# A sigmoid-gate projection computed as four more groups of a seven-product matmul loop, with the residual strips built one stage later

## The chip, the cores and the metric

The kernel runs on one core of a Trainium2 chip. The metric is the device time of one execution in microseconds. A core has a matmul engine (TensorE, PE in the profile; its weight loads are listed as PEld), three engines for element work (VectorE or DVE, ScalarE or ACT, GpSimd or POOL), and SyncE (SP), which here only issues DMAs. Each engine runs its own instructions in order; they wait for one another through semaphores. SBUF is the on-chip memory with 128 partitions, PSUM is the memory that PE writes to, and DRAM lies outside the core.

## What is computed

One step of a one-layer decoder, for a prompt of 512 tokens and 8 single-token samples with the same weights: 520 token columns in all. The input projection, the mLSTM, the window attention and the first LayerNorm end in a vector `x` of 1024 features for each token. What follows is what the change touches:

```python
g, u = jnp.split(x @ w_gate_up, 2, axis=-1)          # 1024 -> 2 x 2816
ffn = (jax.nn.silu(g) * u) @ w_down                  # 2816 -> 1024
ple = jax.nn.sigmoid(x @ w_ple_gate) * (p @ w_ple)   # 1024 -> 1024, the "gate"
x = layer_norm(ALPHA * x + ffn + ple, ln2_g, ln2_b)
```

All data are float32.

## The kernel before

**Layout.** Activations lie with features on the partitions: a matrix of 1024 features is 8 strips of 128 x 520. [...] Each float32 operand is split into a high part (rounded to fp32r by an ACT copy) and a low part (the rest, a DVE subtraction; both in `split`, L216 and L217). A product is three matmuls: high x high, high x low, low x high. The normalised input of this stage is `x1hi`, `x1lo`, in the slabs T0 and T1.

**Weights.** `load_next` (L163) brings weight blocks of up to 1 MB into the ring `raw` of two buffers, from SP's queue; a block's load waits until the buffer's last reader is done. A block of 256 columns is two pieces of 128. `get(k)` returns piece k split, and has pieces k+1 and k+2 split ahead of time into the rings `whi` and `wlo` (3 buffers each).

**The stages at the end, in order.**

1. `w_gate_up`. The first `BSW` = 2 of its 11 column blocks of 256 are done classically (`mm3ab`, L243). The other nine, gate and up part alternating, are the 18 entries of the list `sw`, the groups of the *seven-product loop* (L1703). It treats a group of 256 output rows, 1024 inputs and 520 columns as 2 x 2 blocks, and forms the four output blocks from seven block products instead of eight (`ORDER`: a11, s4, s1, s2, a22, a12, s3). A product is 4 k-blocks x 3 = 12 matmuls of 260 columns (L1600); one step of the loop is one product. Weight blocks come as four loads of 256 KB a group (`st_load`, L176). `w_sum` forms the sums of weight blocks on DVE, `w_hi` and `w_lo` split them (L1579, L1584), `harvest` combines results: ACT seeds a PSUM bank from another, DVE adds two terms (L1689, L1694), and `put_g` or `put_h` takes the finished block. `put_g` applies Silu on ACT (L1618) and keeps the result in the ring `gt` (5 buffers); `put_h` multiplies it with the up part on DVE (L1629) and splits the product into `hhi`, `hlo`, the input of the down projection. Strips 16 to 21 of it can't be split yet: their place is taken by sums of activations that the loop reads (`tf`). They stay unsplit in `h6`, in slab T2.
2. The *gate stage* (L1731), eight row blocks of 128 done classically, 48 matmuls each. For each, ACT takes tanh(z/2) from PSUM (`sig_gate`, L1168), and DVE builds the residual strip `base[f]` in three operations for each half (L1740 to L1742): (tanh + 1) times half of `p @ w_ple`, plus ALPHA x1hi, plus ALPHA x1lo. Half of `p @ w_ple` was written to the DRAM tile `plesc` at the start of the kernel and is brought back by SP (L1729). The six strips of `h6` are split here as well.
3. The *down projection* (L1783). For three blocks b of two output rows each, the 22 input strips are taken in three parts g of 8, 8 and 6 (`KG`), two pieces a each: 18 pieces, then 3 pieces for row 6, then row 7, whose second half is interleaved with the output stage. After a row's last piece `ev_d` adds the strip to PSUM on DVE (L1762), PE transposes the sum (L1771), ACT copies it to `R2` (L1772), and DVE takes statistics (L1780).
4. The output stage: the second LayerNorm over tokens and the stores.

**What sets the order.** Inside `tc.manual_schedule` (the loop, the output stage) the order of PE, DVE, ACT and POOL is that of the program text. Elsewhere, and for SP's queue everywhere, a planner orders each engine's instructions with its own model of time; on the chip every queue then runs strictly in that order. A tile of a ring or slab can be taken when all readers of its predecessor are done.

Of the kernel before, what the change touches and what calls it, by code (L numbers as in the profile page):

```python
# [9 lines left out]
F32 = mybir.dt.float32  # L10
# [7 lines left out]
P = 128  # L18
# [32 lines left out]
def tile_hybrid_step(  # L51
# [25 lines left out]
    def psm():  # L77
        return pm.tile([P, 512], F32, tag="m", name=nm("psm"))
# [7 lines left out]
    def ring(tag, n, bufs, p=P):  # L86
        return wp.tile([p, n], F32, tag=tag, name=nm(tag), bufs=bufs)
# [3 lines left out]
    def slab(i):  # L91
        return up.tile([P, U], F32, tag=f"T{i}", name=nm(f"T{i}_"))
# [4 lines left out]
    def v3(t):  # L97
        t3 = t[:, : KD * NT].rearrange("p (j c) -> p j c", j=KD)
        return [t3[:, j, :] for j in range(KD)]
# [38 lines left out]
    def add_block(src, kc, ncol, pcol=P):  # L138
        bi_ = len(blocks)
        blocks.append((src, kc, ncol))  # L140
        first = len(pieces)
        for a in range(0, ncol, pcol):
            pieces.append((bi_, a, kc, pcol, a + pcol >= ncol))
        return first
# [66 lines left out]
    def get(k, ahead=2):  # L211
        prep_to(k + ahead)
        return ready.pop(k)

    def split(hi, lo, src, le=None):
        S.activation(rr(hi), src, AF.Copy)  # L216
        (le or V).tensor_tensor(rr(lo), src, hi, ALU.subtract)  # L217
# [18 lines left out]
    def mm3ab(pss2, parts, total=None, begin=0):  # L236
        tot = total if total is not None else sum(3 * p[3] for p in parts)
        i = begin
        for hi, lo, wc, kc, ah, al, k0 in parts:
            for k in range(kc):  # L240
                for w, a in ((hi, ah), (hi, al), (lo, ah)):
                    for ps, (c0, n) in zip(pss2, HALVES):
                        T.matmul(  # L243
                            ps[:, :n],
                            rr(w[:, k, wc : wc + P]),
                            rr(a[k0 + k][:, c0 : c0 + n]),
                            start=(i == 0),
                            stop=(i == tot - 1),
                        )
                    i += 1  # L250
        return i
# [41 lines left out]
    for b in range(11):  # L293
        for c0 in (0, DFF):
            src = w_gu2[:, c0 + 256 * b : c0 + 256 * (b + 1)]
            if b < BSW:
                add_block(src, KD, 256)
            else:
                sw.append((src, b, c0 > 0))
    k_sw = len(blocks)  # L300
    blocks.extend([None, None])
    k_pg = len(pieces)
    for b in range(4):
        add_block(w_pg[0][:, 256 * b : 256 * (b + 1)], KD, 256)
    k_dn = len(pieces)
    KG = ((0, 8), (8, 8), (16, 6))
    for b in range(3):
# [85 lines left out]

    pT = [[strip(2 + 2 * i + k) for k in range(2)] for i in range(2)]
    plesc = dp.tile([P, KD, NT], F32, tag="plesc", name="plesc")

    def ple_p():
        for hf, (c0, n) in enumerate(HALVES):
# [767 lines left out]
    def sig_gate(psx, n):  # L1166
        th = ring("th", 264, 3)
        S.activation(th[:, :n], psx[:, :n], AF.Tanh, scale=0.5)  # L1168
        return th
# [244 lines left out]
    def part(w):  # L1414
        return [(w[0], w[1], 0, KD, x1hi, x1lo, 0)]
# [194 lines left out]
    def later(s, kind, f):  # L1610
        todo.setdefault((s, kind), []).append(f)
# [10 lines left out]
    def put_h(s, b, r, hf, src, sc=1.0, own=None):  # L1622
# [7 lines left out]
        if f < 16:  # L1630
            hi, lo = (x[f // 8][f % 8][:, c0 : c0 + TH] for x in (hhi, hlo))
            later(s + 1, "act", lambda: S.activation(rr(hi), h, AF.Copy))
            later(s + 2, "dve", lambda: V.tensor_tensor(rr(lo), h, hi, ALU.subtract))

    pz = {}

    def product(s):
# [17 lines left out]

    def harvest(s):
        g, form = steps[s - 1]
        _, b, up = sw[g]
        put = put_h if up else put_g

        def seed(f):
            later(s, "seed", f)

        if form == "a11":
            pb, pa = pss(), pz[g, "a"]
            pz[g, "b"] = pb
            if g < 2:
                prime(pb)
            seed(lambda: S.activation(pb[:, :TH], pa[:, :TH], AF.Copy))
        elif form == "s1":  # L1670
            p5, pc = ring("th", 264, 3), pz[g, "c"]
            pz[g, "p5"] = p5
            seed(lambda: S.activation(p5[:, :TH], pc[:, :TH], AF.Copy))
        elif form == "s2":
            pb, pd, u1 = pz.pop((g, "b")), psm(), ring("th", 264, 3)
            pz[g, "d"], pz[g, "u1"] = pd, u1
            if g < 2:
                prime(pd)
            seed(lambda: S.activation(pd[:, :TH], pb[:, :TH], AF.Copy))
            seed(lambda: S.activation(u1[:, :TH], pb[:, :TH], AF.Copy))  # L1680
        elif form == "a12":
            put(s, b, 0, 0, pz.pop((g, "a"))[:, :TH])
        elif form == "a22":
            put(s, b, 1, 0, pz.pop((g, "d"))[:, :TH], -1.0)
        else:
            x = ring("tmp", 264, 4) if up else ring("gt", 264, 5)
            xs = x[:, :TH]
            if form == "s3":
                V.scalar_tensor_tensor(  # L1689
                    xs, pz[g, "d"][:, :TH], -1.0, pz.pop((g, "p5"))[:, :TH], ALU.mult, ALU.subtract  # L1690
                )
                put(s, b, 1, 1, xs, own=x)
            else:
                V.tensor_tensor(xs, pz.pop((g, "c"))[:, :TH], pz.pop((g, "u1"))[:, :TH], ALU.add)  # L1694
                put(s, b, 0, 1, xs, own=x)
# [23 lines left out]
            if 0 <= s < ns:  # L1719
                product(s)  # L1720

    base = v3(h5)[6:]
    for k, hx in ((2, hlo), (3, hhi)):
        ta, tb = slab2(k, "h5")
        hx.append([ta[:, i * NT : (i + 1) * NT] for i in range(KF - 16)])
        base += [tb[:, i * NT : (i + 1) * NT] for i in range(2)]
    base += [ring("stg", NT, 2) for _ in range(2)]
    for f in range(KD):
        nc.sync.dma_start(base[f], plesc[:, f, :])  # L1729

    for f in range(KD):  # L1731
        w = get(k_pg + f)
        p2 = (psm(), psm())
        mm3ab(p2, part(w))
        if 1 <= f < 7:
            split(hhi[2][f - 1], hlo[2][f - 1], h6[f - 1])
        for psx, (c0, n) in zip(p2, HALVES):
            th = sig_gate(psx, n)
            bs = base[f][:, c0 : c0 + n]
            V.scalar_tensor_tensor(bs, th[:, :n], 1.0, bs, ALU.add, ALU.mult)  # L1740
            V.scalar_tensor_tensor(bs, x1hi[f][:, c0 : c0 + n], ALPHA, bs, ALU.mult, ALU.add)
            V.scalar_tensor_tensor(bs, x1lo[f][:, c0 : c0 + n], ALPHA, bs, ALU.mult, ALU.add)  # L1742

    R2 = slab(0)[:, : NCH * D].rearrange("p (c d) -> p c d", c=NCH)
    t1n = slab(1)
    ysm = t1n[:NS, :D]
    l2g = t1n[:, D : 2 * D]
    l2b = t1n[:, 2 * D : 3 * D]
    st2 = t1n[:, 3 * D : 3 * D + 192].rearrange("p (c f s) -> p c f s", c=NCH, f=KD)
    RS = t1n[:, 3 * D + 192 : 3 * D + 256].rearrange("p (f b) -> p f b", f=KD)  # L1750
    RQ = t1n[:, 3 * D + 256 : 3 * D + 320].rearrange("p (f b) -> p f b", f=KD)
    rss = t1n[:, 3 * D + 320 : 3 * D + 336].rearrange("p (a b) -> p a b", a=2)
    nc.scalar.dma_start(l2g, ln2_g[0].partition_broadcast(P))
    nc.scalar.dma_start(l2b, ln2_b[0].partition_broadcast(P))

    def dpart(g, w):
        return [(w[0], w[1], 0, KG[g][1], hhi[g], hlo[g], 0)]

    def ev_d(f, hf, psx):
        c0, n = HALVES[hf]  # L1760
        r2 = ring("tmp", 264, 4)
        V.tensor_tensor(r2[:, :n], psx[:, :n], base[f][:, c0 : c0 + n], ALU.add)  # L1762
        if hf == 0:
            G.tensor_copy(RS[:, f, :], r2[:, :NS])  # L1764
        return r2

    def ev_dt(f, hf, r2):
        ps = pss()
        o = NS if hf == 0 else 0
        for i in range(2):  # L1770
            T.transpose(ps[:, i * P : (i + 1) * P], r2[:, o + i * P : o + (i + 1) * P], ident)  # L1771
        S.activation(  # L1772
            R2[:, 2 * hf : 2 * hf + 2, f * P : (f + 1) * P],
            ps[:, : 2 * P].rearrange("p (c d) -> p c d", c=2), AF.Copy,
        )
        return ps
# [6 lines left out]
    for b in range(3):  # L1783
        pps = [(psm(), psm()) for _ in range(2)]
        cnt = [0, 0]
        for g in range(3):
            for a in range(2):
                w = get(kp)
                kp += 1
                cnt[a] = mm3ab(pps[a], dpart(g, w), total=3 * KF, begin=cnt[a])  # L1790
                if g == 2:
                    for hf in range(2):
                        f = 2 * b + a
                        ev_ds(f, hf, ev_dt(f, hf, ev_d(f, hf, pps[a][hf])))
# [11 lines left out]
    for g in range(3):  # L1806
        ws.append(get(kp, 1))
        kp += 1
        cnt = mm3(pa, HALVES[0], dpart(g, ws[g]), total=3 * KF, begin=cnt)

    h0, h1, q3 = slice(0, 512), slice(512, D), slice(768, D)

    def mmb(k0, k1):
# [156 lines left out]
```

## Time and profile before

| | us |
|---|---|
| three timed runs | 897.55, 898.10, 898.61 |
| median | 898.1 |
| the profiled execution | 900.21 |
| its span, first to last instruction | 898.2 |
| mean granted PE clock | 0.99 |

| stage, in the span | from | to |
|---|---|---|
| seven-product loop, on PE | 525 | 709 |
| gate stage, on PE | 705 | 753 |
| down projection | 753 | 875 |
| output stage | 875 | 898 |

(The loop's last product and the gate stage's first matmuls are interleaved on PE.) In the profile, L12 is line 12 of the kernel. A row of instructions gives line, engine, operation, output and input by their names, shape and count, then busy time and mean length; in brackets stands how long the engine was idle before and who ended that. A row of stretches gives for each engine the busy time and in brackets the number of instructions. A list of waits gives total, number and longest.

### The profile page before, as it was taken

The page shows a single profiled execution, that of the slowest core. Times are in us where ns is not written, and L with a number is a line of the kernel's source. Part 1 is how long each engine was busy: PE and PEld are TensorE (multiplying, and loading weights), DVE is VectorE, ACT ScalarE, POOL GpSimd, SP SyncE. Part 2 cuts the span into 40 slices and gives each one's busy share as a digit, 9 for nine tenths or more (in the row PEclk, how much of TensorE's full clock was granted, in tenths as well). Part 3 has the DMA queues.
Part 4 walks back from the last instruction along what each step waited for, and adds up shares of the span by engine and source line. Part 5 has one row for each costly group of instructions (what it writes and reads, how often), then busy time and mean ns, then how long its engine had stood idle before and what let it go on. Part 6 is the DMA issues. An engine that isn't in the chain of part 4 may idle for free.

```text
span 898.2 us, 18486 instructions
## 1 busy us (share of the span) xinstructions
PE 873.0 (97%) x7130; PEld 860.3 (96%) x7130; DVE 637.4 (71%) x1547; ACT 466.6 (52%) x1102; POOL 159.2 (18%) x320
## 2 busy tenths in 40 slices
PE   8999899999999999999999999999999999999994
PEld 7999899999999899999999999999999999999993
DVE  7788555688888777778877978999988654223327
ACT  6545254657777655557326656666665522212212
POOL 5441321115464411311014100000000000000004
PEclk9999999999999999999999999999999999999997
DMA  7642631336465441121710333333332723322212
GB/s 240 212 151 71 188 102 54 55 112 148 144 174 169 142 141 49 53 90 48 235 48 1 90 100 100 101 114 107 99 106 73 229 87 123 103 94 71 66 41 96
DMA packets 118039, 99.42 MB, mean 111 GB/s; under 512 B 6410, under 2 KB 112610, under 8 KB 117928
## 3 DMA queue, kind: packets, MB, share of 16 engines
q1 hardware_dynamic: 117520, 96.94, 36.0%
q8 instruction: 56, 0.92, 0.4%
q10 hardware_dynamic: 432, 1.31, 0.4%
q14 instruction: 31, 0.25, 0.1%
HBM read 89.01 MB, written 10.34 MB: 111 GB/s over the span
## 4 chain that ended last, share of the span: by engine, by line
PE 85%; DVE 6%; DMA 3%; ACT 3%; issue 1%; POOL 1%; SPq 0%; DVEq 0%; ACTq 0%; POOLq 0%
PE psm L243 46%; PE psm L1600 12%; PE pss L1600 9%; PE psm L226 6%; PE pss L683 2%; DMA big<-vsd 1%; PE psm L467 1%; PE pss L736 1%; PE pss L720 1%; PE psm L1428 1%; PE pss L1069 1%; PE pss L1073 1%; ACT T L1371 1%; DMA out_dram<-stg 1%; DMA T<-in_w_ple_dram 1%
## 5 line engine op out<-in xcount | busy, mean ns | idle before, releaser
L243 PE MATMUL psm<-T,whi 128*128 128x264 f32 x2000 | 346.5, 286 | 0.6 <-DVE Qbd L670 0.4
L243 PEld LDWEIGHTS psm<-T,whi 128*128 128x128 f32 x2000 | 284.7, 189 | 2.6 <-PE pss L1147 0.6
L243 PE MATMUL psm<-T,wlo 128*128 128x264 f32 (+1 forms) x1056 | 230.0, 288 | 1.5 <-DVE wlo L217 1.5
L217 DVE TENSOR_TENSOR wlo<-raw,whi 128x1024 fp32r<-128x1024 f32 (+1 forms) x86 | 104.8, 1218 | 107.2 <-ACT whi L216 106.8
L243 PEld LDWEIGHTS psm<-T,wlo 128*128 128x128 f32 x1056 | 168.1, 189 | 2.4 <-DVE wlo L217 1.7
L216 ACT ACTIVATE whi<-raw 128x1024 fp32r<-128x1024 f32 (+1 forms) x86 | 89.1, 1038 | 154.5 <-PE psm L243 139.6
L1764 POOL COPY T<-tmp 128x8 f32<-128x8 f32 x8 | 1.5, 190 | 376.4 <-DVE tmp L1762 376.4
L708 POOL TENSOR_SCALAR g<-g,sm 128x256 f32<-128x256 f32 (+1 forms) x64 | 36.2, 578 | 80.3 <-DVE sm L706 24.2
L243 PE MATMUL psm<-L,whi 128*128 128x264 f32 x224 | 45.0, 282 | 0.0
L701 ACT ACTIVATE g<-g,sm 128x256 f32<-128x256 f32 (+1 forms) x64 | 30.2, 474 | 19.3 <-DVE sm L697 18.2
L217 POOL TENSOR_TENSOR gt<-big,gt 128x256 fp32r<-128x256 f32 x32 | 27.5, 868 | 55.2 <-ACT gt L216 36.1
L1584 DVE TENSOR_TENSOR whi<-raw,whi 128x512 fp32r<-128x512 f32 x45 | 30.9, 687 | 8.5 <-ACT whi L1579 7.6
L1579 ACT ACTIVATE whi<-raw 128x512 fp32r<-128x512 f32 x45 | 28.3, 628 | 15.9 <-PE psm L1600 12.8
L1579 ACT ACTIVATE wlo<-raw 128x512 fp32r<-128x512 f32 x45 | 28.3, 630 | 13.6 <-ACT gt L1618 8.8
L243 PEld LDWEIGHTS psm<-L,whi 128*128 128x128 f32 x224 | 34.3, 188 | 0.0
L1584 DVE TENSOR_TENSOR wlo<-raw,wlo 128x512 fp32r<-128x512 f32 x45 | 30.9, 686 | 3.7 <-ACT wlo L1579 3.3
L1600 PE MATMUL psm<-tf,whi 128*128 128x260 f32 x228 | 30.3, 282 | 0.0
L692 DVE CUSTOM_DVE_ANT_0 g<-pss,amaskA,sink 128x256 f32<-128x256 f32 (+1 forms) x64 | 26.1, 444 | 4.0 <-PE pss L683 2.5
L1600 PE MATMUL psm<-T,wlo 128*128 128x260 f32 x216 | 28.9, 283 | 0.0
L1600 PE MATMUL pss<-tf,whi 128*128 128x260 f32 x216 | 28.9, 283 | 0.0
L1600 PE MATMUL pss<-tf,wlo 128*128 128x260 f32 x216 | 28.9, 283 | 0.0
L1600 PE MATMUL psm<-T,whi 128*128 128x260 f32 x216 | 28.9, 283 | 0.0
(446 smaller groups left out, 2007.8 us busy)
## 6 DMA issues: line engine op xcount, KB each, us to landing
raw<-in_w_in_dram SPq DMA_DIRECT2D x24, 1024.0 KB
raw<-in_w_gate_up_dram SPq DMA_DIRECT2D x72, 256.0 KB
raw<-in_w_down_dram SPq DMA_DIRECT2D x6, 1024.0 KB
big<-in_state_mlstm_C_dram SPq DMA_DIRECT2D x8, 512.0 KB
big<-vsd SPq DMA_DIRECT2D x8, 512.0 KB
out_dram<-big SPq DMA_DIRECT2D x8, 512.0 KB
raw<-in_w_out_dram SPq DMA_DIRECT2D x4, 1024.0 KB
raw<-in_w_gate_up_dram SPq DMA_DIRECT2D x4, 1024.0 KB
```

Of the source, the lines that this page charges most:

```text
L216: S.activation(rr(hi), src, AF.Copy)
L217: (le or V).tensor_tensor(rr(lo), src, hi, ALU.subtract)
L226: T.matmul(ps[:, :n], rr(w[:, k, wc : wc + P]), rr(a[k0 + k][:, c0 : c0 + n]), start=(i == 0), stop=(i == tot - 1),)
L243: T.matmul(ps[:, :n], rr(w[:, k, wc : wc + P]), rr(a[k0 + k][:, c0 : c0 + n]), start=(i == 0), stop=(i == tot - 1),)
L467: T.matmul(t01[t][hf][:, :n], rr(w[:, k, :]), rr(x[k][:, c0 : c0 + n]), start=(k == 0 and i == 0), stop=(k == KD - 1 and i == 2),)
L683: T.matmul(sc[:, a, :w], rr(q[:, a, n * P : (n + 1) * P]), rr(KS[:, kv, hl, (n - 1 + k0) * P : (n + 1) * P]), start=(hl == 0), stop=(hl == 1),
L692: V.tensor_tensor_reduce(out=pr[:, a, :w], in0=sc[:, a, :w], in1=amaskA[:, k0 * P :], scale=1.0, scalar=sink8[:, 2 * j + a : 2 * j + a + 1 ...
L701: S.activation(pr[:, a, :w], pr[:, a, :w], AF.Exp, bias=sm[:, 2 + a : 3 + a], scale=ASC, accum_out=sm[:, 8 + a : 9 + a],)
L708: G.tensor_scalar(pr[:, a, :w], pr[:, a, :w], sm[:, 12 + a : 13 + a], 0.5, ALU.mult, ALU.mult)
L1579: S.activation(rr(t[:, 0]), wsrcs[i], AF.Copy)
L1584: V.tensor_tensor(rr(lo), wsrcs.pop(i), hi, ALU.subtract)
L1600: T.matmul(ps[:, :TH], rr(w[:, j, :]), rr(x[j]), start=(start and j == 0 and i == 0), stop=(j == 3 and i == 2), skip_group_check=not start,)
```

## The change

The four column blocks of `w_ple_gate` are no longer pieces of a classical stage. They are groups 18 to 21 of the seven-product loop, with a third way of taking a finished block, `put_p`: tanh on ACT into a buffer of the ring `gt`, then a DMA from SP into a new DRAM tile `thsc`. The gate stage is gone. The strips are built in the down projection by `mkbase`, ahead of the matmuls of a piece that the table `bases` names (i counts pieces 0 to 17): tanh and `plesc` are loaded for each half, then the same three DVE operations follow. The splits of `h6` come ahead of pieces 0 to 2. Since `x1hi` and `x1lo` are read longer, `R2` moves from slab T0 to T2, the rows of the second LayerNorm are loaded to T1 at piece 12 by SP instead of ACT, the statistics move to `amaskA`, and the strips get other buffers (four of the late tiles, four of the ring `gt`, two of `stg`).

```diff
-                sw.append((src, b, c0 > 0))
+                sw.append((src, b, int(c0 > 0)))
+    for b in range(4):
+        sw.append((w_pg[0][:, 256 * b : 256 * (b + 1)], b, 2))
     k_sw = len(blocks)
     blocks.extend([None, None])
-    k_pg = len(pieces)
-    for b in range(4):
-        add_block(w_pg[0][:, 256 * b : 256 * (b + 1)], KD, 256)
...
+    thsc = dp.tile([P, KD, NT], F32, tag="thsc", name="thsc")
...
+    def put_p(s, b, r, hf, src, sc=1.0, own=None):
+        t = own or ring("gt", 264, 5)
+        f, c0 = 2 * b + r, hf * TH
+
+        def tanh():
+            S.activation(t[:, :TH], src, AF.Tanh, scale=0.5 * sc)
+            nc.sync.dma_start(thsc[:, f, c0 : c0 + TH], t[:, :TH])
+
+        later(s if own is None else s + 1, "act", tanh)
...
-        _, b, up = sw[g]
-        put = put_h if up else put_g
+        _, b, kind = sw[g]
+        put = (put_g, put_h, put_p)[kind]
...
-            x = ring("tmp", 264, 4) if up else ring("gt", 264, 5)
+            x = ring("tmp", 264, 4) if kind == 1 else ring("gt", 264, 5)
...
-    base = v3(h5)[6:]
+    strips = []
     for k, hx in ((2, hlo), (3, hhi)):
         ta, tb = slab2(k, "h5")
         hx.append([ta[:, i * NT : (i + 1) * NT] for i in range(KF - 16)])
-        base += [tb[:, i * NT : (i + 1) * NT] for i in range(2)]
-    base += [ring("stg", NT, 2) for _ in range(2)]
-    for f in range(KD):
-        nc.sync.dma_start(base[f], plesc[:, f, :])
-
-    for f in range(KD):
-        w = get(k_pg + f)
-        p2 = (psm(), psm())
-        mm3ab(p2, part(w))
-        if 1 <= f < 7:
-            split(hhi[2][f - 1], hlo[2][f - 1], h6[f - 1])
-        for psx, (c0, n) in zip(p2, HALVES):
-            th = sig_gate(psx, n)
-            bs = base[f][:, c0 : c0 + n]
-            V.scalar_tensor_tensor(bs, th[:, :n], 1.0, bs, ALU.add, ALU.mult)
+        strips += [tb[:, i * NT : (i + 1) * NT] for i in range(2)]
+    gts = [[ring("gt", 264, 5) for _ in range(2)] for _ in range(2)]
+    strips += gts + [ring("stg", NT, 2) for _ in range(2)]
...
+    def mkbase(f):
+        for hf, (c0, n) in enumerate(HALVES):
+            th = ring("th", 264, 3)[:, :n]
+            bs = base(f, hf)
+            nc.sync.dma_start(th, thsc[:, f, c0 : c0 + n])
+            nc.sync.dma_start(bs, plesc[:, f, c0 : c0 + n])
+            V.scalar_tensor_tensor(bs, th, 1.0, bs, ALU.add, ALU.mult)
             V.scalar_tensor_tensor(bs, x1hi[f][:, c0 : c0 + n], ALPHA, bs, ALU.mult, ALU.add)
             V.scalar_tensor_tensor(bs, x1lo[f][:, c0 : c0 + n], ALPHA, bs, ALU.mult, ALU.add)
 
-    R2 = slab(0)[:, : NCH * D].rearrange("p (c d) -> p c d", c=NCH)
-    t1n = slab(1)
...
-    nc.scalar.dma_start(l2g, ln2_g[0].partition_broadcast(P))
-    nc.scalar.dma_start(l2b, ln2_b[0].partition_broadcast(P))
+    bases = {2: (0,), 3: (1,), 5: (2,), 6: (3,), 7: (4,), 8: (5,), 9: (6,), 10: (7,)}
...
+    def late_rows():
+        t1n = slab(1)
...
+        nc.sync.dma_start(late_r["g"], ln2_g[0].partition_broadcast(P))
+        nc.sync.dma_start(late_r["b"], ln2_b[0].partition_broadcast(P))
...
                 w = get(kp)
                 kp += 1
+                i = 6 * b + 2 * g + a
+                for j in range(2 * i, 2 * i + 2) if i < 3 else ():
+                    split(hhi[2][j], hlo[2][j], h6[j])
+                for j in bases.get(i, ()):
+                    mkbase(j)
+                if i == 12:
+                    late_rows()
                 cnt[a] = mm3ab(pps[a], dpart(g, w), total=3 * KF, begin=cnt[a])
                 if g == 2:
+                    if "R2" not in late_r:
+                        late_r["R2"] = slab(2)[:, : NCH * D].rearrange("p (c d) -> p c d", c=NCH)
                     for hf in range(2):
                         f = 2 * b + a
                         ev_ds(f, hf, ev_dt(f, hf, ev_d(f, hf, pps[a][hf])))
```

More of the change, by code (lines that the diff above doesn't have):

```diff
@@ new lines, in tile_hybrid_step, with base @@
+    gts = [[ring("gt", 264, 5) for _ in range(2)] for _ in range(2)]
+    strips += gts + [ring("stg", NT, 2) for _ in range(2)]
+    def base(f, hf):
+        c0, n = HALVES[hf]
+        return strips[f][hf][:, :n] if f in (4, 5) else strips[f][:, c0 : c0 + n]
+    def mkbase(f):
[5 more added lines that the diff above has]
+            V.scalar_tensor_tensor(bs, th, 1.0, bs, ALU.add, ALU.mult)
@@ L1741, in tile_hybrid_step @@
             V.scalar_tensor_tensor(bs, x1hi[f][:, c0 : c0 + n], ALPHA, bs, ALU.mult, ALU.add)
             V.scalar_tensor_tensor(bs, x1lo[f][:, c0 : c0 + n], ALPHA, bs, ALU.mult, ALU.add)
-    R2 = slab(0)[:, : NCH * D].rearrange("p (c d) -> p c d", c=NCH)
-    t1n = slab(1)
[L1746 to L1750, printed above, removed]
@@ L1751, in tile_hybrid_step @@
-    RQ = t1n[:, 3 * D + 256 : 3 * D + 320].rearrange("p (f b) -> p f b", f=KD)
-    rss = t1n[:, 3 * D + 320 : 3 * D + 336].rearrange("p (a b) -> p a b", a=2)
-    nc.scalar.dma_start(l2g, ln2_g[0].partition_broadcast(P))
-    nc.scalar.dma_start(l2b, ln2_b[0].partition_broadcast(P))
+    bases = {2: (0,), 3: (1,), 5: (2,), 6: (3,), 7: (4,), 8: (5,), 9: (6,), 10: (7,)}
+    st2 = amaskA[:, :192].rearrange("p (c f s) -> p c f s", c=NCH, f=KD)
+    RS = amaskA[:, 192:].rearrange("p (f b) -> p f b", f=KD)
@@ new lines, in tile_hybrid_step @@
+    late_r = {}
+    def late_rows():
+        t1n = slab(1)
+        late_r["ysm"] = t1n[:NS, :D]
+        late_r["g"] = t1n[:, D : 2 * D]
+        late_r["b"] = t1n[:, 2 * D : 3 * D]
+        late_r["RQ"] = t1n[:, 3 * D : 3 * D + 64].rearrange("p (f b) -> p f b", f=KD)
+        late_r["rss"] = t1n[:, 3 * D + 64 : 3 * D + 80].rearrange("p (a b) -> p a b", a=2)
+        nc.sync.dma_start(late_r["g"], ln2_g[0].partition_broadcast(P))
+        nc.sync.dma_start(late_r["b"], ln2_b[0].partition_broadcast(P))
@@ L1761, in ev_d @@
         r2 = ring("tmp", 264, 4)
-        V.tensor_tensor(r2[:, :n], psx[:, :n], base[f][:, c0 : c0 + n], ALU.add)
+        V.tensor_tensor(r2[:, :n], psx[:, :n], base(f, hf), ALU.add)
         if hf == 0:
@@ L1772, in ev_dt @@
         S.activation(
-            R2[:, 2 * hf : 2 * hf + 2, f * P : (f + 1) * P],
+            late_r["R2"][:, 2 * hf : 2 * hf + 2, f * P : (f + 1) * P],
             ps[:, : 2 * P].rearrange("p (c d) -> p c d", c=2), AF.Copy,
@@ L1809, in tile_hybrid_step @@
         cnt = mm3(pa, HALVES[0], dpart(g, ws[g]), total=3 * KF, begin=cnt)
+    R2 = late_r["R2"]
+    ysm, l2g, l2b, RQ, rss = (late_r[n] for n in ("ysm", "g", "b", "RQ", "rss"))
     h0, h1, q3 = slice(0, 512), slice(512, D), slice(768, D)
```

## The prediction

> **What bounds the kernel now.** I read the page first (busy shares), then the stretches of time of the last 375 us, the chain of work over the stage that goes, the timeline around one harvest in the down projection, and the lists of waits.
>
> ```profile
> span 898.2 us, 18486 instructions
> PE 873.0 (97%) x7130; PEld 860.3 (96%) x7130; DVE 637.4 (71%) x1547; ACT 466.6 (52%) x1102; POOL 159.2 (18%) x320
> ```
>
> ```profile
> 605.00:665.00 60.00, 60.00 (x503) 60.00 (x502) 54.42 (x102) 40.04 (x89) 0.00 (x0) 1.00 0.37 106
> 705.50:753.10 47.60, 47.60 (x398) 47.60 (x397) 29.71 (x61) 15.34 (x28) 0.00 (x0) 1.00 0.38 127
> 753.10:781.00 27.90, 27.90 (x235) 27.90 (x234) 8.05 (x13) 5.96 (x8) 0.00 (x0) 1.00 0.34 116
> ```
>
> Columns: stretch, length, then busy time and instructions of PE, PEld, DVE, ACT and POOL, the granted clock, the DMA share and GB/s. The first row lies inside the seven-product loop, the second is the gate stage, the third the first pieces of the down projection. In all three PE is busy for the whole length at clock 1.00, and PE's own list of waits between 523 and 870 us is empty. So in this part of the kernel time is the number of matmuls times their pace, and nothing else ends last. DVE is nearly full in the loop (54.42 of 60 us) and nearly idle in the down projection (8.05 of 27.9).
>
> The chain of work over the same place:
>
> ```profile
> 679.78 5.75 PE psm L1600 x48
> 685.53 4.33 PE pss L1600 x36
> 689.86 5.75 PE psm L1600 x48
> ...
> 707.37 1.45 PE psm L1600 x12
> 708.82 74.58 PE psm L243 x621
> ```
>
> One group of the loop is 48 + 36 = 84 matmuls in 5.75 + 4.33 = 10.08 us, 120.0 ns each, and the next begins at once. The classical matmuls of L243 run at 74.58 us / 621 = 120.1 ns. Both forms cost the same per matmul, so only the count decides.
>
> **The change part by part.**
>
> *Matmuls removed.* Gate before: 8 row blocks x 8 k x 3 products x 2 halves = 384 matmuls, 384 x 120.1 ns = 46.1 us. That fits the stretch of 47.60 us, in which the loop's last 12 matmuls (1.45 us) lie too. Gate after: 4 groups x 84 = 336, 4 x 10.08 = 40.3 us; the extra priming matmul of a bank is made only for the first two groups, so none is added. Difference: **-5.8 us**, all on the path.
>
> A rule of the Trainium skill gives another size for this term. "TensorE: Matmul & The Clock Gate", section "Back-to-back issue gap", gives N/2.4 + 2.5 ns for an isolated matmul, 110.8 ns at 260 columns; by this estimate 48 fewer would be worth 5.3 us and end at 892.8. The same section warns that this leaves out the weight load. The trace disagrees by 9 ns a matmul, and I keep the trace's pace.
>
> *Vector work in the four added groups.* Per group DVE makes 7 low parts and 4 sums of 128x512 and 2 harvests; the gate blocks have no product with a second factor and no split of a result.
>
> ```profile
> L1584 DVE TENSOR_TENSOR whi<-raw,whi 128x512 fp32r<-128x512 f32 x45 | 30.9, 687 | 8.5 <-ACT whi L1579 7.6
> 679.78:689.86 10.08, 10.08 (x87) 10.08 (x86) 8.57 (x17) 5.80 (x12) 0.00 (x0) 1.00 0.19 54
> ```
>
> 11 x 0.687 + 2 x 0.42 = 8.4 us in a group of 10.08; the second row is one whole group with 8.57 us of DVE and 5.80 of ACT beneath a full PE. An ACT tanh takes the place of an ACT silu of the same shape. I take 0. The cover is PE's 10.08 us; 1.7 us of it is spare.
>
> *Tanh to DRAM.* 16 stores of 128x260 (133 KB) from SP. Each holds a buffer of the ring gt (5 buffers, 4 taken a group) until it has landed. Going through the seven-step order, the same buffer is wanted again after 8 steps at the earliest, 8 x 10.08 / 7 = 11.5 us. No store of this shape is in the trace. The nearest row is an engine that waited for a store to free its buffer; a second one shows waits on data read back from DRAM:
>
> ```profile
> ACT stg L983 <- DMA out_dram<-stg: 5.0, 1, 5.0
> ACT big L1140 <- DMA big<-vsd: 10.7, 5, 4.4
> SPq L176 <- DVE L L1633: 27.8, 11, 4.2
> ```
>
> (Total, number, longest.) Tanh comes up to 2 steps (2.9 us) after the buffer is taken, the store at worst 5.0 us later: 7.9 us, less than 11.5. I take 0. The other end: SP stands behind a weight load whose buffer isn't free (third row, 4.2 us), 12.1 us in all, 0.6 us too late, with DVE 4 steps (5.8 us) ahead of PE as a second cover. If that cover is lost in every group, one step of 1.44 us goes per group, +5.8 us in all.
>
> *SP's queue.* Added: 16 stores, 16 reloads of tanh, 16 half reloads of plesc in place of 8 whole ones, 16 weight loads of 256 KB in place of 4 of 1 MB, and the two rows of the second norm, which leave ACT's queue. At 0.37 us an issue (the row below) the 54 extra cost SP about 20 us over 160 us. SP was waiting for buffers most of that time, so 0; late issues are in the bounds of the next part.
>
> *Strips in the down projection.* The 48 vector operations are the same as before (three per half strip, 422 ns in the first row below), and so are the six splits of h6. They leave the gate stage, where DVE had room, for pieces 0 to 10 of the down projection.
>
> ```profile
> L1740 DVE SCALAR_TENSOR_TENSOR h<-th,h 128x264 f32<-128x264 f32 (+1 forms) x8 | 3.1, 422 | 0.0
> L217 DVE TENSOR_TENSOR h<-T,h 128x520 fp32r<-128x520 f32 x6 | 4.1, 694 | 0.2
> 777.24 1.23 DVE L217 TENSOR_TENSOR wlo<-raw,whi 128x1024 fp32r<-128x1024 f32 x1 [4.96 <-ACT whi L216]
> 780.58 0.76 DVE L1762 TENSOR_TENSOR tmp<-psm,T 128x264 f32<-128x264 f32 x2 [2.12 <-PE psm L243]
> 784.07 0.89 DVE L1780 BATCH_NORM_STATS2 T<-pss 128x6 f32<-128x128 f32 x4 [1.29 <-ACT T L1772]
> 783.24 0.38 PE L1771 MATMUL pss<-ident,tmp 128*128 128x128 f32 x2
> 738.14 0.37 SPq L163 DMA_DIRECT2D raw<-in_w_down_dram  x1
> 740.00:741.00 1.00, 1.00 (x10) 1.00 (x9) 0.15 (x1) 0.00 (x0) 0.00 (x0) 1.00 1.07 381
> ```
>
> A piece is 48 x 120.1 ns = 5.77 us (6-deep ones 4.33). The fullest, pieces 5 and 6, want a split of 1.23, a strip of 6 x 0.42 = 2.5 and a harvest of 0.76 + 0.89: 5.4 us. The two pieces last 4.33 + 5.77 = 10.1 us and want 10.8, so DVE falls 0.7 us behind once; weight splits run two pieces (some 10 us) ahead of PE, which covers it. DMA: per block of 1 MB come two strips of 540 KB, 2.1 MB in 11.5 us, 183 GB/s of the 381 that the last row shows. Not full.
>
> What has no such lead is the harvest itself. DVE adds the strip to PSUM at 780.58 and PE's transposes of it stand at 783.24: from the end of the first add (780.58 + 0.42) PE's order leaves 2.2 us. With four gates between an in-order DVE and PE (the harvests of rows 0 to 3, which end with pieces 4, 5, 10 and 11), a strip operation that waits for its reload ahead of a harvest passes anything over 2.2 us on to PE. Lower bound 0: there is no PE wait left to win back in this stretch. Upper bound per place: the longest reload wait, 4.4, behind a 1 MB load in the same queues, 1 MB / 381 GB/s = 2.8, less 2.2: 5.0 us, 20 us for four. I take 0, since the buffers of strips 0 to 3 come free with the loop's last product, five pieces (4 x 5.77 + 4.33 = 27 us) before the first harvest, and the plesc reloads of before made nobody wait.
>
> The Trainium skill speaks against the round trip: "DMA: Bandwidth & Descriptors", section "Anatomy of one DMA", puts a fixed 2.0 us on each DMA beside bytes / 436 GB/s, most of it the receipt of the last write. For a 135 KB reload this is an estimate of 2.3 us, 0.1 us over the margin, 0.4 us at four places, 892.7. The trace's waits reach 4.4 us, so it doesn't speak for so small a tail.
>
> *Boundary of loop and down projection.* The first three weight pieces are prepared in the loop's last three steps as for the gate before; their size is the same. hhi[2] is first read at piece 4. The rows of the second norm are wanted only after piece 23 and loaded at piece 12. I take 0.
>
> **Sum.** 898.2 - 5.8 = 892.4 us of span. The profiled execution took 900.21 us, 2.0 around the span, and would take 894.4. The three timed runs have a median of 898.1, within 0.1 of the span, so the forecast is 898.1 - 5.8 = **892.3 us**.
>
> **Rivals.**
>
> *A. Part of it is handed back at harvests.* One or two of the four places wait a typical reload, 10.7 / 5 = 2.1 us, behind a 1 MB load (2.8): 4.9 - 2.2 = 2.7 us each; one place, 895.0. For: in-order queues, and DVE is never free for long at pieces 5 and 6. Against: reloads can be issued long before.
>
> *B. Slower.* SP issues the block load first and the reloads behind it, at pieces 5, 7, 9 and 11 (a block's last piece is split two ahead of an odd one), so that DVE stands at strips when rows 0 to 3 are to be harvested; the upper price of 5.0 us holds at three of the four places: +15.0, 907.3. It turns the sign from the point where the four together pass 5.8 us, and makes it slower by more than 0.2% from 7.6 us, so two places at full price do it. Against: margin and early buffers, as above. For: SP's own waits from 690 to 860 us,
>
> ```profile
> SPq L163 <- DVE wlo L217: 103.7, 12, 11.1
> ```
>
> up to 11.1 us for a weight buffer's release, and whatever stands behind such a wait is late.
>
> *C. The stores reach the loop*, one step lost in each added group: -5.8 + 5.8, 898.1, no change.
>
> *D. It doesn't do what it says.* If a group were set by DVE and not by PE, fewer matmuls would save nothing. The group with 8.57 of 10.08 us of DVE excludes it; I give it no chance of its own.
>
> **How the numbers follow.** Forecast (892.3, give or take 1) 0.66; A 0.20, of which 0.04 ends within 0.2% (two places, 897.7); C 0.05; B 0.09. This kernel can be told from no change at about 0.2%, 1.8 us. Faster 0.66 + 0.16 = 0.82; same 0.04 + 0.05 = 0.09; slower 0.09. Range: below 892.3 there is only the scatter of runs (0.5 us each way); above it takes in one place of A with that scatter and some of the second, and leaves out C and B: 891.5 to 896.2.
>
> **What would show it.** Right: the loop has 22 groups of 10.08 us, the down projection starts 40.3 us after the old end of group 18, PE's list of waits stays empty, and L1771 has no wait on the adds before the last row. A or B: PE's L1771 waits for the add (L1762) at rows 0 to 3, with DVE waiting on a DMA of thsc or plesc just ahead. C: DVE or ACT waiting on the DMA into thsc inside the loop, with groups over 10.08 us. A down projection longer than before without such waits would make the whole reading wrong.

## The result, and the profile after

| | median us | lowest to highest | runs |
|---|---|---|---|
| before | 898.1 | 897.55 to 898.61 | 5 |
| changed | 892.83 | 890.85 to 894.93 | 5 |

The ratio is 0.9944, with an interval of 0.9925 to 0.9964: the change saves 0.56%, with an interval of 0.36 to 0.75%. The profiled execution took 894.93 us, 2.0 more than its span. First the page of the changed kernel:

```profile
span 892.9 us, 18610 instructions
PE 866.8 (97%) x7082; PEld 854.0 (96%) x7082; DVE 658.9 (74%) x1591; ACT 480.6 (54%) x1138; POOL 160.5 (18%) x320
```

PE has 7082 matmuls instead of 7130, the 48 fewer of the sum. The chain of work in the added groups shows the same rhythm as the old ones:

```profile
718.27 5.75 PE psm L1600 x48
724.01 4.33 PE pss L1600 x36
728.34 5.75 PE psm L1600 x48
```

From one group to the next it is 728.34 - 718.27 = 10.07 us. The stretches of the changed kernel (columns as before; the end of the loop with the first pieces of the down projection, and the two stretches after it):

```profile
705.50:748.00 42.50, 41.88 (x347) 41.47 (x346) 30.10 (x51) 27.17 (x59) 0.00 (x0) 1.00 0.50 154
748.00:775.00 27.00, 27.00 (x227) 27.00 (x226) 21.65 (x53) 7.42 (x11) 0.00 (x0) 1.00 0.81 249
775.00:803.00 28.00, 27.07 (x227) 26.86 (x226) 11.49 (x24) 5.31 (x8) 0.51 (x2) 1.00 0.42 134
```

Before, PE was busy for every microsecond of this part. Now the weight loads (PEld) lack 42.50 - 41.47 = 1.03 us in the first row and 28.00 - 26.86 = 1.14 in the third. The list of waits of PE's weight loads between 508 and 848 us says for whom (the kernel before has nothing in its list between 509 and 853 us):

```profile
PEld pss L1785 <- DVE tmp L1776: 1.1, 1, 1.1
PEld psm L243 <- DVE wlo L217: 0.7, 1, 0.7
PEld psm L243 <- ACT whi L216: 0.3, 1, 0.3
```

(L1785 and L1776 of the changed kernel are the transposes and the adds of the harvest, L1771 and L1762 before.) So the first harvest hands back 1.1 us, and the boundary of loop and down projection 0.7 + 0.3.

**A yardstick.** Two rows of the chain of work fence the whole change: A, the start of the classical gate and up matmuls just ahead of the loop, and B, the start of row 6 in the down projection. From the kernel before and the changed one:

```profile
508.06 17.28 PE psm L243 x142
853.76 12.99 PE psm L243 x108
```

```profile
506.25 17.28 PE psm L243 x142
848.37 12.99 PE psm L243 x108
```

B - A fell from 345.70 to 342.12, by 3.58 us. The profiled executions differ by 900.21 - 894.93 = 5.28 us. Of the rest, 1.81 lie ahead of A, where nothing was changed: up to A, every engine has the same instructions in the same order. What lies behind B differs by less than 0.2 us.

### The profile page after: what moved, and what is told of

Same layout as the page of the kernel before. It is cut to its first block, busy times and chain, and to the rows that moved or that the text cites. A ratio compares the mean times of both kernels' runs of the same rounds, so it can differ in the third digit from the quotient of the medians.

```text
span 892.9 us, 18610 instructions
## 1 busy us (share of the span) xinstructions
PE 866.8 (97%) x7082; PEld 854.0 (96%) x7082; DVE 658.9 (74%) x1591; ACT 480.6 (54%) x1138; POOL 160.5 (18%) x320
## 4 chain that ended last, share of the span: by engine, by line
PE 77%; DVE 10%; DMA 5%; ACT 3%; issue 2%; POOL 1%; SPq 1%; DVEq 0%; ACTq 0%; POOLq 0%
PE psm L243 36%; PE psm L1600 14%; PE pss L1600 10%; PE psm L226 6%; DMA big<-vsd 2%; DVE wlo L217 1%; PE pss L736 1%; PE psm L467 1%; PE pss L683 1%; PE pss L720 1%; PE psm L1428 1%; DMA thsc<-gt 1%; DMA wdb<-bcd 1%; ACT T L1371 1%; PE pss L1069 1%
## 5 line engine op out<-in xcount | busy, mean ns | idle before, releaser
L243 PE MATMUL psm<-T,whi 128*128 128x264 f32 (+1 forms) x1744 | 304.3, 286 | 0.7 <-DVE Qbd L670 0.4
L243 PEld LDWEIGHTS psm<-T,whi 128*128 128x128 f32 x1744 | 248.5, 188 | 2.9 <-issue 0.8
L243 PE MATMUL psm<-T,wlo 128*128 128x256 f32 (+1 forms) x928 | 203.2, 288 | 2.0 <-DVE wlo L217 2.0
L217 DVE TENSOR_TENSOR wlo<-raw,whi 128x1024 fp32r<-128x1024 f32 (+1 forms) x78 | 94.6, 1213 | 76.0 <-ACT whi L216 75.3
L243 PEld LDWEIGHTS psm<-T,wlo 128*128 128x128 f32 x928 | 147.8, 188 | 3.1 <-DVE wlo L217 2.5
L216 ACT ACTIVATE whi<-raw 128x1024 fp32r<-128x1024 f32 (+1 forms) x78 | 80.6, 1035 | 120.6 <-PE psm L243 108.4
L1584 DVE TENSOR_TENSOR whi<-raw,whi 128x512 fp32r<-128x512 f32 x55 | 37.8, 687 | 11.7 <-ACT whi L1579 10.8
L1584 DVE TENSOR_TENSOR wlo<-raw,wlo 128x512 fp32r<-128x512 f32 x55 | 37.7, 686 | 6.0 <-ACT wlo L1579 5.6
L1600 PE MATMUL psm<-tf,whi 128*128 128x260 f32 x276 | 36.7, 281 | 0.0
L1600 PEld LDWEIGHTS psm<-tf,whi 128*128 128x128 f32 x276 | 34.5, 188 | 0.0
```

The costliest lines, as they stand in the source:

```text
L243: T.matmul(ps[:, :n], rr(w[:, k, wc : wc + P]), rr(a[k0 + k][:, c0 : c0 + n]), start=(i == 0), stop=(i == tot - 1),)
L1584: V.tensor_tensor(rr(lo), wsrcs.pop(i), hi, ALU.subtract)
L1600: T.matmul(ps[:, :TH], rr(w[:, j, :]), rr(x[j]), start=(start and j == 0 and i == 0), stop=(j == 3 and i == 2), skip_group_check=not start,)
```

## The experiments

My theory H after this first look: the 48 matmuls are worth their full price; two waits hand part of it back; and the time ahead of A scatters, so that total times can't separate edits of 1 us, while B - A can. Its rivals: a slower pace of the loop or of the matmuls themselves (then B - A stays short of the full price with no wait in the list); for the boundary, the order of SP's queue, or a load that lands late. All traces in one table, A, B - A and span in us; "boundary" and "harvest" are PE's waits in its list between A and B. "Time" is the median of the timed runs of that row, with the ratio to the kernel before, run beside it.

| kernel | A | B - A | span | boundary | harvest | time | ratio |
|---|---|---|---|---|---|---|---|
| before | 508.06 | 345.70 | 898.2 | none | none | 898.1 | |
| before_again | 504.38 | 345.72 | 894.5 | none | none | 896.56 (one run) | |
| changed, first trace | 506.25 | 342.12 | 892.9 | 1.0 | 1.1 | 892.83 | 0.9944 |
| changed_again | 504.01 | 341.13 | 889.8 | none | 1.3 | 892.17 | 0.9963 (0.9946 to 0.998) |
| changed_third | 501.97 | 341.31 | 887.8 | 0.3 | 1.2 | 892.89 | 0.9953 (0.9932 to 0.9974) |
| stores_on_act | 503.86 | 341.12 | 889.9 | 1.0 | none | 894.08 | 0.998 (0.9961 to 0.9999) |
| harvest_first | 504.29 | 339.87 | 888.7 | none | none | 890.81 | 0.994 (0.9921 to 0.996) |
| both_edits | 503.97 | 340.53 | 889.4 | 0.6 | none | 891.34 | 0.9951 (0.9933 to 0.9968) |
| slots_swapped | 502.69 | 339.83 | 887.1 | none | none | 890.58 | 0.9932 (0.9912 to 0.9952) |
| harvest_and_slots | 503.33 | 339.82 | 887.7 | none | none | 892.87 | 0.995 (0.9931 to 0.997) |
| harvest_and_slots_again | 506.12 | 339.81 | 890.5 | none | none | 891.12 | 0.994 (0.9916 to 0.9963) |
| strips_only | 506.21 | 345.72 | 896.3 | none | none | 897.32 | 1.0008 (0.9992 to 1.0024) |

Between traces of one kernel A moves by up to 4.3 us. B - A does not: 345.70 and 345.72 for the kernel before, 339.81 to 339.87 for the four with the change and without a wait. Where a wait stands in the list, B - A is longer by its length, within 0.3 us. The span behind B is 44.4 to 44.9 us in every trace.

### The changed kernel and the one before, taken again

No edit: `changed_again`, `changed_third`, `before_again`.

> The changed kernel once more, nothing edited. Theory H (handed back): of the 5.8 us that 48 matmuls are worth, 2.2 us come back in every execution, 1.0 us where the loop meets the down projection (PE waits for the split of the first down weights) and 1.1 us at the first harvest (PE's transposes wait for DVE's add). Then both waits are in this trace again, within half a microsecond, and the PE work from the start of the loop to the end of the down projection is again 3.6 us shorter than before. Theory N (scatter): the two waits belong to that one execution; here they are under 0.5 us in sum and that stretch is 5.8 us shorter. On the 1.8 us by which the loop began earlier than in the kernel before, though no instruction ahead of it was reordered: if that is scatter between executions, the loop's start lies elsewhere here, by a microsecond or more, between 521 and 527 us of the span.

> The kernel before, nothing edited, for a second trace of it. In its first trace the last classical matmuls ahead of the loop began at 508.1 us, in five traces of edited kernels, in which no instruction ahead of the loop is ordered otherwise, at 503.9 to 506.3. If that is scatter between executions, the kernel before shows a start below 507 here too; if the change itself shortens the part ahead of the loop, it shows 508 again. The stretch from there to row 6 is 345.7 us again, within 0.3.

> The changed kernel a third time, beside the edited one on the same chip. By the traces so far its stretch from the last classical gate and up matmuls to row 6 is 341.1 or 342.1 us: the harvest wait of 1.1 to 1.3 us is there each time, the boundary's wait of 1.0 us in one of two. Expected: a stretch of 340.9 to 342.2 us with a harvest wait of 1 to 1.5 us. If the harvest wait is absent, it isn't a cost of every execution.

The harvest wait came in all three executions of the changed kernel (1.1, 1.3, 1.2 us). The boundary wait came in two, at 1.0 and 0.3: it hangs on how fast a DMA lands, as a later part shows. The expectation that both waits come in every execution held for the harvest alone. B - A was 342.12, 341.13 and 341.31, 3.6 to 4.6 us below the 345.7 of before. In the second trace of the kernel before A was 504.38, 3.68 us earlier than in its first, with B - A the same to 0.02: the scatter lies in the part that nobody touched.

### Is SP's queue what makes the boundary late?

```diff
-            nc.sync.dma_start(thsc[:, f, c0 : c0 + TH], t[:, :TH])
+            nc.scalar.dma_start(thsc[:, f, c0 : c0 + TH], t[:, :TH])
```

> The 16 stores of tanh are issued from ACT's queue instead of SP's. Theory H says that the first load of down weights came 1.4 us later (counted from the loop's end) than the gate's first load did before, because it stood in SP's queue behind a reload and a store that waited for tanh. Without the stores in that queue it is issued at least 1 us earlier, the boundary's wait of 1.0 us goes, and the time falls by about 1 us against the changed kernel. Rival: the wait comes from the DMA engines being busy at that place (up to 380 GB/s), so the load lands as late as before and the wait stays.

The timeline at the end of the loop, of the changed kernel and of `stores_on_act`: the issue of the first load of a down weight block (1 MB), the start of the loop's last product s4, and ACT's split of that block's first piece.

```profile
735.83 0.39 SPq L163 DMA_DIRECT2D raw<-in_w_down_dram  x1
...
742.55 1.61 PE L1600 MATMUL pss<-T,wlo 128*128 128x260 f32 x12
743.15 1.06 ACT L216 ACTIVATE whi<-raw 128x1024 fp32r<-128x1024 f32 x1 [2.88 <-DMA raw<-in_w_down_dram]
```

```profile
733.47 3.22 SPq L163 DMA_DIRECT2D raw<-in_w_down_dram  x2
...
740.19 1.61 PE L1600 MATMUL pss<-T,wlo 128*128 128x260 f32 x12
740.79 1.06 ACT L216 ACTIVATE whi<-raw 128x1024 fp32r<-128x1024 f32 x1 [2.89 <-DMA raw<-in_w_down_dram]
```

In both the load is issued 6.72 us ahead of that product, and ACT stands 2.9 us before it lands. With tanh's stores off SP's queue nothing came earlier, so the queue's order is not the limit. This theory fell. The time didn't fall by the expected 1 us either: the median was 894.08, and 892.17 for the changed kernel in the same job, though both have the same B - A. (The harvest wait went as well, though only just. The planner ordered the strips otherwise, with 41 instead of 46 of their 48 operations ahead of the first add; both halves of row 0 were added in one go from 774.87, and PE's transposes began at 775.35.)

### What frees the buffer

The same place in the kernel before, with the DVE instruction that ends just ahead of the issue:

```profile
694.09 0.68 DVE L1569 TENSOR_TENSOR raw<-raw,raw 128x512 f32<-128x512 f32 x1
694.80 0.37 SPq L163 DMA_DIRECT2D raw<-in_w_ple_gate_dram  x1
...
701.68 1.05 ACT L216 ACTIVATE whi<-raw 128x1024 fp32r<-128x1024 f32 x1
...
704.07 1.61 PE L1600 MATMUL pss<-T,wlo 128*128 128x260 f32 x12
```

Here the load goes out 704.07 - 694.80 = 9.27 us ahead of the last product, when a *sum* of weight blocks (L1569) is done, and ACT waits for nothing. In the changed kernel it goes out at 735.83, after this row:

```profile
735.06 0.69 DVE L1584 TENSOR_TENSOR whi<-raw,whi 128x512 fp32r<-128x512 f32 x1
```

That is a *split*, a later step. (In `stores_on_act` the load also goes out 0.1 us after that split, at the same 6.72 us.) `st_load` puts the four blocks of a group into eight places of the two `raw` buffers, by the group's number modulo 2 and 3 (L172, L173). The old last group is 17 and has only a11 in the first buffer, which is free once the sum for s3 is made. The new last group is 21; a11, a12 and a22 lie in the first buffer and a21 in the second, so neither is empty, and the first load comes behind a split. So the first load goes out 9.27 - 6.72 = 2.55 us later against the last product. (The 1.4 us of the expectation above were counted from the end of the loop.) `slots_swapped` exchanges two places in the table, so that group 21 has all four blocks in the first buffer and the second is empty; the first loads follow:

```diff
-        x = (0, 1, 4, 2, 5, 3, 6, 7)[i]
+        x = (0, 1, 4, 5, 2, 3, 6, 7)[i]
...
-            ((0, "a11"), (0, "a21"), (0, "a22"), (0, "a12")),
-            ((1, "a22"), (1, "a21"), (1, "a11"), (2, "a22")),
+            ((0, "a11"), (0, "a22"), (0, "a12"), (1, "a21")),
+            ((0, "a21"), (1, "a22"), (1, "a11"), (2, "a22")),
```

> The changed kernel with two places of the weight buffers exchanged: the a21 blocks of odd groups lie in the first raw buffer, those of even groups in the second. Theory S (slots): the first load of down weights comes late because the last group's blocks then lie in both raw buffers (group 21 takes other places than group 17 did), so that the first buffer to come free does so two loop steps later than in the kernel before (by the program, after the low part of step ns-3, which runs four steps ahead, and not after the sum that reads a11). With the exchange all of the last group's blocks lie in one buffer, the load is issued about 2 steps (2 to 3 us) earlier against the end of the loop, ACT no longer waits for its landing, and the boundary's wait (0 to 1.1 us in the traces so far) is gone. Rival D (engines busy): the load lands late because reloads and stores fill the DMA engines there; then ACT waits for it still. The harvest wait of 1.1 to 1.3 us stays in either case, so the time is at most 1 us below the changed kernel, which its scatter may hide.

Timeline of `slots_swapped`:

```profile
729.15 0.38 SPq L163 DMA_DIRECT2D raw<-in_w_down_dram  x1
...
736.64 1.05 ACT L216 ACTIVATE whi<-raw 128x1024 fp32r<-128x1024 f32 x1
...
739.02 1.61 PE L1600 MATMUL pss<-T,wlo 128*128 128x260 f32 x12
```

The load now goes out 739.02 - 729.15 = 9.87 us ahead, 3.15 earlier than in the changed kernel; ACT has no wait and starts 2.38 us ahead of the product, as in the kernel before (704.07 - 701.68 = 2.39). The boundary wait is gone. My expectation for the harvest was wrong: its wait went too (below).

The late issue only takes the spare time away; how long the load then takes decides what PE feels. In the six traces with the change and the old places the load is issued 6.71 or 6.72 us ahead of the last product, and ACT stands waiting for it each time:

| kernel | from the issue to ACT's split, us | boundary wait, us |
|---|---|---|
| changed_again | 6.19 | none |
| harvest_first | 6.21 | none |
| changed_third | 6.48 | 0.3 |
| both_edits | 6.84 | 0.6 |
| changed, first trace | 7.32 | 1.0 |
| stores_on_act | 7.32 | 1.0 |

The DMA engines are busy there each time (a share of 0.90 to 0.95 in the 6 us behind the issue), so the rival of busy engines may well be the source of this scatter of 1.1 us; no run isolates it. With the load issued 9.87 us ahead it no longer reaches PE.

### What stands ahead of the first harvest

DVE's timeline in the changed kernel, up to the add of row 0 (L1776). A strip is built in two halves, of 264 and 256 columns, with three operations each: 48 in all. The strips of rows 0 to 3 lie in slabs (`h`), those of 4 and 5 in `gt`, those of 6 and 7 in `stg`:

```profile
758.33 1.10 DVE L1750 SCALAR_TENSOR_TENSOR h<-th,h 128x256 f32<-128x256 f32 x3
...
765.08 0.77 DVE L1750 SCALAR_TENSOR_TENSOR h<-th,h 128x264 f32<-128x264 f32 x2 [2.41 <-DMA th<-thsc]
...
772.75 0.43 DVE L1750 SCALAR_TENSOR_TENSOR stg<-th,stg 128x264 f32<-128x264 f32 x1 [0.56 <-DMA th<-thsc]
...
776.29 0.76 DVE L1752 SCALAR_TENSOR_TENSOR stg<-T,stg 128x256 f32<-128x256 f32 x2
...
777.30 0.42 DVE L1776 TENSOR_TENSOR tmp<-psm,h 128x264 f32<-128x264 f32 x1
```

and PE just behind it:

```profile
777.78 0.44 PE L1785 MATMUL pss<-ident,tmp 128*128 128x128 f32 x2 [0.93 <-DVE tmp L1776]
```

The program text names pieces 2 to 10 for the strips. The planner has put 46 of the 48 operations ahead of the first add, down to those of rows 6 and 7, whose sums are due tens of microseconds later. The strips' buffers are free early, so they didn't hold them back. DVE, which stood idle 2.41 + 0.56 us for reloads in between, comes to the due add too late. `harvest_first` ties the strips from row 2 on to the add of row 1:

```diff
+    evd = {}
...
-        V.tensor_tensor(r2[:, :n], psx[:, :n], base(f, hf), ALU.add)
+        evd[f, hf] = V.tensor_tensor(r2[:, :n], psx[:, :n], base(f, hf), ALU.add).ins
...
-    bases = {2: (0,), 3: (1,), 5: (2,), 6: (3,), 7: (4,), 8: (5,), 9: (6,), 10: (7,)}
+    bases = {2: (0,), 3: (1,), 6: (2,), 7: (3,), 8: (4,), 9: (5,), 10: (6,), 11: (7,)}
...
-                    mkbase(j)
-                if i == 12:
+                    after(mkbase, j, f_=[evd[1, 1]]) if j > 1 else mkbase(j)
+                if i == 13:
```

> DVE's strip operations for rows 2 to 7 are put behind the adds of rows 0 and 1; strips 0 and 1 stay ahead. Theory H: the wait of PE's transposes at the first harvest (1.1 us) goes, no new one comes at rows 2 and 3, and the time falls by about 1 us against the changed kernel. Rival: the strips squeezed into pieces 6 to 11 delay weight splits or the adds of rows 2 and 3, so that the wait only moves there and the time stays or rises.

Now 12 of the 48 operations stand ahead of the first add. The harvest wait is gone, no other came, B - A is 339.87, and the boundary happened to hold in this execution (6.21 us in the table above). The median, 890.81, is 1.4 us below that of the changed kernel in the same job. Together with the store edit:

> Both edits together. Theory H: both waits go, the whole 5.8 us stay, about 2 us below the changed kernel, near 890.5 to 891. Theory N: no difference from the changed kernel beyond the scatter of its runs.

B - A was 340.53 with 0.6 us at the boundary: the harvest stays mended, the boundary does not, so theory H held for one wait of the two.

In `slots_swapped` the harvest came in time although 47 of the 48 operations are still ahead. Its timeline, DVE and then PE:

```profile
771.44 0.75 DVE L1776 TENSOR_TENSOR tmp<-psm,h 128x264 f32<-128x264 f32 x2
```

```profile
772.11 0.38 PE L1785 MATMUL pss<-ident,tmp 128*128 128x128 f32 x2
```

Two adds in 0.75 us put the end of the first near 771.44 + 0.42 = 771.86, 0.25 us before PE's turn. It is just in time. DVE begins the strips 9.4 us after the start of the last product, against 11.9 in the changed kernel's first trace and 10.7 in the other two, and the reload for the seventh half strip made it wait 1.7 us instead of 2.4. That the earlier weight load is what let DVE begin earlier is an argument; no run tests it alone.

### Both mends, and the strips alone

`harvest_and_slots` has the diffs of `slots_swapped` and `harvest_first`.

> Strip operations of rows 2 to 7 behind the adds of rows 0 and 1, and the exchanged places. Both theories of waits together: no PE wait between the loop's start and row 6, the stretch from the last classical gate and up matmuls to row 6 of the down projection 5.8 us shorter than before (339.9 us against 345.7), the time 5.5 to 6 us below the kernel before in the same job.

> The version with both edits again. Theory: its stretch is 339.8 us in each execution, since the first load of down weights has 2.5 us to spare and the adds of rows 0 and 1 don't stand behind the strips of later rows; it is 1.2 to 2.3 us shorter than the changed kernel's. The median time is lower than the changed kernel's by about as much, 0.1 to 0.25%, if the scatter ahead of the loop (3.7 us between two executions of the kernel before) averages out over the rounds, which it may not.

B - A was 339.82 and 339.81, with no wait. The full worth of the removed matmuls is so 345.71 - 339.82 = 5.89 us, and the changed kernel keeps 3.6 to 4.6 of it. The medians, 892.87 and 891.12, beat the kernel before, but their lowest to highest (889.71 to 894.34, 888.62 to 895.45) overlap with the changed kernel's (889.19 to 895.61, run beside the second of them). The first is 4.0 us below the kernel before in its job, and not 5.5 to 6 as expected; the second is 1.8 below the changed kernel. The scatter of single runs covers the 1.3 to 2.3 us that B - A finds between them.

`strips_only` keeps the gate stage classical and moves only the strips:

```diff
-    for b in range(4):
-        sw.append((w_pg[0][:, 256 * b : 256 * (b + 1)], b, 2))
...
+    k_pg = len(pieces)
+    for b in range(4):
+        add_block(w_pg[0][:, 256 * b : 256 * (b + 1)], KD, 256)
...
+    for f in range(KD):
+        w = get(k_pg + f)
+        p2 = (psm(), psm())
+        mm3ab(p2, part(w))
+        for psx, (c0, n) in zip(p2, HALVES):
+            th = sig_gate(psx, n)
+            nc.sync.dma_start(thsc[:, f, c0 : c0 + n], th[:, :n])
```

> Half of the change: the gate stays classical (384 matmuls, after the loop of 18 groups), its tanh goes to DRAM, and the strips are built in the down projection as in the changed kernel. Theory H: moving the strips gains nothing and costs the harvest wait, so the stretch is 345.7 us plus 0 to 1.3 us and the time equal to the kernel before or up to 1.5 us above it; the whole gain of the change is the 48 matmuls. Rival: part of the gain comes from the strips' leaving the gate stage; then this kernel is faster than before by a microsecond or more.

B - A is 345.72 and the ratio 1.0008 (0.9992 to 1.0024): moving the strips gains nothing and costs nothing, not even the harvest wait that I expected. The whole gain is that of the matmuls. Here all 48 strip operations stand ahead of the first add, with the same reloads, and PE's list of waits between A and B is empty: DVE begins the first add at 778.95, and PE's transposes follow at 781.41 without waiting. So the order of the strips alone doesn't make the harvest late. It takes both: work that isn't due ahead of work that is (`harvest_first` takes that away), and too little time for DVE to get through it, which I put down to the loop's new end.

## Why the prediction was right, and where not

**Matmuls: right.** Predicted 5.8 us, all on the path; 5.89 once nothing is handed back. The Trainium skill's formula ("TensorE: Matmul & The Clock Gate", section "Back-to-back issue gap") would have made it 5.3; the traces disagree by 0.6 us, as the pace of before's trace did.

**Vector work and stores in the added groups: right.** The groups last 10.07 us, and no list of waits names a store into `thsc`. Rival C, which loses a step in each group, is excluded by that period.

**Strips move: right that the move itself is free**, shown by `strips_only`. The step "I take 0" for the harvests was wrong in size: rival A happened, at one place, with 1.1 to 1.3 us instead of 2.7. By my own signs this was A's: PE's transposes waited for the add, with DVE's waits for `thsc` ahead. The reason I gave against it, that the buffers of strips 0 to 3 come free early, holds and is part of the cause: so do those of 4 to 7, and the planner used them, ahead of the first harvest. The other reason, that reloads can be issued long before, fails: tanh comes back through the ring `th` of three buffers, so a reload has to wait until DVE has read the one three places before it. The seventh, issued at 759.51, could not go out before DVE's fourth read had ended (758.33 + 0.42 = 758.75). I counted the operations by the pieces at which the text names them, and not by the order in which the engine would get them. I looked for the crowd at pieces 5 and 6; it stood ahead of the harvest that ends piece 4. Rows 1 to 3 had no wait. Rival B, slow at three places, did not come.

The Trainium skill's 2.0 us and 436 GB/s ("DMA: Bandwidth & Descriptors", section "Anatomy of one DMA") gave an estimate of 2.3 us for such a reload. That section's fit is for DMAs that GpSimd issues, and SP issues these, so it was no firm bound. Here the seventh to ninth of the 16 reloads of tanh were issued between 759.51 and 761.01, by this row of SP's timeline in the changed kernel:

```profile
759.51 1.50 SPq L1748 DMA_DIRECT2D th<-thsc  x3
```

DVE's seventh half strip began at 765.08, after a wait of 2.41 us for a reload of tanh. That is over 4 us from issue to use, in a stretch that moved 249 GB/s. The direction of the estimate was right and its size too small here.

**Boundary: wrong.** "The first three weight pieces are prepared in the loop's last three steps as for the gate before" is true of their size and their order, but not of when their buffer comes free. That changed with the number of the last group, 17 to 21. Price: 1.0, 0 and 0.3 us in three executions, by how long the load took.

**The sum: right in the median, partly by luck.** The forecast of 892.3 was 0.5 us off, though 1.3 to 2.3 us of its 5.8 were handed back: 898.1 less the 3.6 to 4.6 that B - A shows would be 893.5 to 894.5. In that comparison the kernel before stood high (898.1; 895.89, 896.46 and 896.86 in the later ones), and the profiled executions differ by 1.81 us ahead of A. The scatter "0.5 us each way" was the other step that failed: medians of the unedited changed kernel agree to 0.7 us (892.17 to 892.89), but single runs go from 889.19 to 896.88. In its three traces A alone goes from 501.97 to 506.25, and from 501.97 to 508.06 over all traces. By B - A the change is worth 3.6 to 4.6 us, and the ratios of the three comparisons, 0.9944, 0.9953 and 0.9963, are 3.3 to 5.0 us.

**What stays open:** what moves A by up to 6 us between executions of the same instructions was not traced. Part of it is there early: the first long run of classical matmuls in the chain of work (27.45 us) begins anywhere from 38.06 to 41.70 us. How often the boundary wait comes is known from three executions of the changed kernel, and why its load takes 6.2 to 7.3 us is open. What makes DVE late at the first harvest, beside the order of the strips, was argued from traces and not isolated.

## What to carry to other kernels

When work is moved into a stage whose queues a planner fills, look at what stands ahead of the first operation that is due there: here work with free buffers and no deadline was put in front. When a loop gets a different number of turns, work out again which rotating buffer its last turn holds and when the next stage's first load gets it. When single runs scatter by more than an edit can bring, compare the length of the stage between two fixed points of the trace.

## What the hardware showed that I had not expected

A stretch of 340 us in which PE never waits repeats to 0.02 us (345.70 and 345.72 in the kernel before, 339.82 and 339.81 with both mends), while the 500 us ahead of it, with the same instructions in the same order, end anywhere from 501.97 to 508.06. And a reload of 135 KB took over 4 us from issue to use where the traffic was 249 GB/s.
